# A two-layer encoder trunk: inputs reordered with products of constants ahead of them, right-hand sums made in the up-projections, and late splits of the down-projections put far behind their loads

## The chip, the cores and the metric

The kernel runs on one core of a Trainium2 chip, in one launch. The metric is the device time of that launch in microseconds. A core has five engines with a queue each: PE (TensorE, matmuls), DVE (VectorE), ACT (ScalarE), POOL (GpSimd) and SP (SyncE, which here only issues transfers). An instruction waits at the head of its engine's queue until its inputs are there, and all that stands behind it waits too. Sixteen DMA engines carry the transfers.

## The reference, cut

Two layers over 1024 frames of width 1024, in float32. Each layer adds a mixer and then a gated MLP to the residual stream x. The mixer of layer 0 is stick-breaking attention beside trailing means, that of layer 1 a gated linear recurrence. What the change touches is the beginning of layer 0's mixer (the projection to q and k) and the MLP of both layers:

```python
def conv_ffn(h, w_up, conv_w, conv_b, w_down):
    u = h @ w_up
    up = jnp.pad(u, ((0, 0), (CONV_WIDTH - 1, 0), (0, 0)))
    conv = conv_b
    for j in range(CONV_WIDTH):
        conv = conv + conv_w[j] * up[:, j:j + s]
    a, g = jnp.split(conv, 2, axis=-1)
    return (jax.nn.silu(a) * g) @ w_down

for layer in range(DEPTH):
    x = x + mixer(rms_norm(x, ...), ...)
    x = x + conv_ffn(rms_norm(x, ffn_norm[layer]), ...)
```

`w_up` is 1024 x 5632 and `w_down` 2816 x 1024.

## The kernel before

Activations are kept transposed, channels on the 128 partitions and frames along a row. Every operand of a product is split into a high part (a cast to a shorter format, done by ACT) and a low part (what the cast lost, subtracted by DVE), and every product is three matmuls: high by high, high by low, low by high. Matmuls are 512 columns wide as a rule. The order on PE is the order of the code. On the other engines a scheduler sets it, by its own estimate of time; in the down-projections SP's order too is that of the code.

**The start.** x comes in eight slices of 128 channels. `Norm.add` (L256) splits each one (`h_hi` on ACT, `h_lo` on DVE) and adds its square to `nacc`. `load_split` (L113) fetches the weights of q and k in two halves each, casts (L139) and subtracts (L140, here on POOL). `start_qk` (L765) multiplies slice by slice: twelve matmuls a slice, 96 in all, to four banks. Then `norm.stats` (L286) sums `nacc`, and the projection to the values follows (L417 to L419).

**The up-projections.** 44 tiles of 128 channels in 22 pairs (a, g); a scheme with seven half-size products instead of eight (`winograd`, L880) computes both tiles of a pair. A pair takes seven products P1 to P7 of 12 matmuls each (line L936). DVE empties the banks (L990, L995, L1001, L1005), scales (L964), runs two steps of the convolution (L1039, L1041), forms the next weights' sums (L907 to L910) and subtracts the low parts (L918). The results of two pairs make one block row of the down-projection's right side: `even` holds the first, `ca` the second. B11 and T1 are stored in DRAM after the first pair; B21, B22, T3 (B22 less B12, L1184) and U (B11 less B21, L1183) after the second.

**The down-projections** (`down`, L1199) use the same scheme: products P1, P5, P6, P3, P7, P4, in that order, of eleven steps (j) each, 66 in all, and then a last part with plain products for B21. A step is twelve matmuls at L1266 to four banks. `prep` (L1243) gets a step's operands three steps ahead (`LEAD`): `fetched` loads the right side into `rb` (four buffers), `left` gets the weights (`rs`, `rw`, `ra`) with a sum on DVE where the scheme wants one (L1226, L1229, L1235), and `split_block` (L1193) casts on ACT (L1195) and subtracts on DVE (L1196). The right sides of P6 and P4 are sums, T3 + B11 and T3 + U: `fetched` loads the first one and then POOL issues a second transfer that adds the other one in place (L1213). The last part needs plain weights (`last_left`, called in P6 at j = 2 and 6, and again in the last part) and plain B21 blocks (`last_right`, from P7's j = 8 on); both load and split in one go.

```python
        right = {"P1": ("B11",), "P5": ("T1",), "P6": ("T3", "B11"), "P3": ("B22",), "P7": ("T3",), "P4": ("T3", "U")}
```

Of the kernel before, what the change touches and what calls it, by code (L numbers as in the profile page):

```python
# [12 lines left out]
F32 = mybir.dt.float32  # L13
R32 = mybir.dt.float32r
AF = mybir.ActivationFunctionType
ALU = mybir.AluOpType
# [24 lines left out]
FGROUP = 2  # L41

# [15 lines left out]
def trunk_kernel(  # L58
# [53 lines left out]

    def load_split(src, pool=None, tags=("whi", "wlo", "wraw"), eng=None, nb=2, raw=None, parts=None,  # L113
                   fetched=None):
        srcs = src if isinstance(src, list) else [src]
        n = sum(a.free_size() for a in srcs)
        pool = pool or wpool
        if fetched is not None:
            raw = fetched
        elif raw is None:  # L120
            raw = (pool if len(tags) > 2 else wpool).tile([P, n], F32, tag=tags[2] if len(tags) > 2 else "wraw",
                                                      name="wraw", bufs=2 if "draw" in tags else 1)
        hi = pool.tile([P, n], R32, tag=tags[0], name="whi", bufs=nb)
        lo = pool.tile([P, n], R32, tag=tags[1], name="wlo", bufs=nb)

        def fetch(cs):
            if not isinstance(src, list):
                nc.sync.dma_start(raw[:, cs], src[:, cs])
# [7 lines left out]
        def part(cs):  # L136
            if fetched is None:
                fetch(cs)
            S.copy(hi[:, cs], raw[:, cs])  # L139
# [111 lines left out]
    class Norm:  # L251
        def __init__(self, gain_col, acc_tile, sq_tile, add_eng=None):
            self.col, self.acc_tile, self.sq_tile = gain_col, acc_tile, sq_tile
            self.h, self.add_eng, self.n = [None] * KT, add_eng, 0

        def add(self, x, parts=None, k=None):  # L256
            k = self.n if k is None else k
            self.n += 1
            hi = hpool.tile([P, T], R32, tag="h", name="h_hi")
            lo = hpool.tile([P, T], R32, tag="h", name="h_lo")  # L260
            g = pcol(self.col + k)
            for cs in parts or [slice(0, T)]:
                a = S.activation(hi[:, cs], x[:, cs], AF.Copy, scale=g)
                b = V.scalar_tensor_tensor(lo[:, cs], x[:, cs], g, hi[:, cs].bitcast(F32), op0=ALU.mult,  # L264
                                           op1=ALU.subtract)
            self.last = a.ins, b.ins
            self.h[k] = hi, lo
            if self.n == 1:
                self.acc = self.acc_tile()
                S.activation(self.acc, x, AF.Square)  # L270
                return
            sq = self.sq_tile()
            S.activation(sq, x, AF.Square)
            (self.add_eng or (V if self.n == KT else G)).tensor_tensor(self.acc, self.acc, sq, op=ALU.add)
# [77 lines left out]
    G.memset(ones, 1.0)  # L352
    epsc = const.tile([P, 1], F32, name="epsc")
# [29 lines left out]
    norm = Norm(C_MIXE, lambda: slot(F32, "nacc"), lambda: etile("kl"), V)  # L383
    for k in range(KT):
        xt = slot(F32, "xt")
        if k == 0:
# [18 lines left out]
    def values(half):  # L405
        wt = [load_split(wv[half, c], ep if half == 0 else None, ("ath", "atl") if half == 0 else ("whi", "wlo"))
              for c in range(2)]
# [158 lines left out]
    def pool_in(g, then):  # L566
# [3 lines left out]
        nc.sync.dma_start(praw[g], poolw[g])  # L570
# [209 lines left out]
    v0 = values(0)  # L780
# [230 lines left out]
    def ffn(layer, nm, after, ow, mixt, onward=None):  # L1011
# [107 lines left out]
        for i in range(FT):  # L1119
# [61 lines left out]
            else:  # L1181
# [3 lines left out]
                b2, ut3 = (dram.tile([P, T], F32, tag=f"{n}{layer}_{i}", name=n) for n in ("b2", "ut3"))  # L1185
                nc.sync.dma_start(b2, ca)
                nc.sync.dma_start(ut3, cg)
                blocks[-1].update(B21=b2[:, T0], B22=b2[:, T1], U=ut3[:, T0], T3=ut3[:, T1])
# [4 lines left out]
    def split_block(src):  # L1193
        t = hpool.tile([P, T], R32, tag="h", name="blk")
        S.copy(t[:, 0:512], src)  # L1195
        V.tensor_sub(t[:, 512:T], src, t[:, 0:512].bitcast(F32))  # L1196
        return t

    def down(layer, blocks, ready, after, onward):  # L1199
# [9 lines left out]
        def fetched(tag, src, add=None, bufs=4):  # L1209
# [30 lines left out]

        right = {"P1": ("B11",), "P5": ("T1",), "P6": ("T3", "B11"), "P3": ("B22",), "P7": ("T3",), "P4": ("T3", "U")}

        def prep(n, j):  # L1243
            if n == "P1" and j < len(ready):
                return ready[j]
            rb = fetched("rb", *(blocks[j][b] for b in right[n]))
# [28 lines left out]
        def last_right(js):  # L1275
            raw = hpool.tile([P, T], R32, tag="h", name="b21").bitcast(F32)
            for cs, j in zip(HALVES, js):
                nc.sync.dma_start(raw[:, cs], blocks[j]["B21"])
                hi = dn.tile([P, 512], R32, tag="ra", name="b21h", bufs=NJ)
                lo = dn.tile([P, 512], R32, tag="rs", name="b21l", bufs=NJ)  # L1280
                S.copy(hi, raw[:, cs])
                V.tensor_sub(lo, raw[:, cs], hi.bitcast(F32))
                b21.append((hi, lo))
# [3 lines left out]
        def last_left(r):  # L1287
            parts = []
            big = (hpool, ("wraw", "h", "h"), (1, 16, 16)) if r == KT // 2 - 1 else (wpool, ("wraw", "whi", "wlo"), (1, 2, 2))
            for k0, k1, (pool, tags, nb) in ((0, KT, big), (KT, NJ, (dn, ("r3", "r3h", "r3l"), (1, 2, 2)))):  # L1290
                raw, hi, lo = ((wpool if t == "wraw" else pool).tile([P, (k1 - k0) * P], d, tag=t, name=t, bufs=b)
                               for t, d, b in zip(tags, (F32, R32, R32), nb))
                nc.sync.dma_start(raw.rearrange("p (f k) -> p f k", k=P), odd[:, k0:k1, r * P:(r + 1) * P])
                S.copy(hi, raw)
                V.tensor_sub(lo, raw, hi.bitcast(F32))
                parts += [(hi[:, sl], lo[:, sl]) for sl in (slice(k * P, (k + 1) * P) for k in range(k1 - k0))]
            return parts
# [8 lines left out]
        rows = {}  # L1306
        for i, (n, j) in enumerate(order):
# [37 lines left out]
        for r in range(half):  # L1345
# [4 lines left out]
            if r + 2 < half:  # L1350
                rows[r + 2] = last_left(r + 2)
# [383 lines left out]
```

## Time and profile before

| | |
|---|---|
| three runs | 2197.35, 2199.06, 2202.14 us (median 2199.06) |
| the profiled execution | 2199.35 us; span from first to last instruction 2197.7 us |
| PE, DVE, ACT, POOL busy | 98%, 76%, 50%, 7% of the span |
| moved by DMA | 280.31 MB, 128 GB/s on average |
| first matmul of the start, first matmul of the norm after q and k | 5.95 us, 31.86 us |
| steps of the down-projections | 881.36 to 1071.43 us (layer 0), 1968.50 to 2162.59 us (layer 1) |

A timeline row has an instruction's start, its length, its engine (a q behind the name is the engine's queue), its line, its operation, what it writes and reads, and in brackets how long the engine had stood idle before it and what ended that. Matmul ends are modelled, so their starts are the safer numbers. A window row has its stretch and length, then each engine's busy time with the number of instructions (PE, PEld, DVE, ACT, POOL), the granted TensorE clock, the busy share of the DMA engines and GB/s. A group row has the number of instructions, their busy time and mean length in ns, then the idle time before them and what ended it. A source row has minimum, median and maximum length in ns, then first and last start.

### The profile page before, as it was taken

The numbers are of one execution on the slowest core, as the hardware profiler recorded it, in microseconds if no ns is written. First come the engines' busy times: TensorE is split into PE (matmuls) and PEld (weight loads), VectorE is DVE, ScalarE is ACT, GpSimd is POOL, SyncE is SP. The second block draws the span as 40 slices with busy tenths as digits, with TensorE's granted clock in tenths as the row PEclk, the third lists the DMA queues.
The fourth block names the chain that finished last, engine by engine and source line by source line (L and its number), as shares of the span: only waits on it lengthen the run. The fifth ranks groups of instructions, "written<-read, shape, count | busy, mean of one in ns | idle before, by whom it ended". The sixth has DMA issues, their size and how long they took to land.

```text
span 2197.7 us, 28082 instructions
## 1 busy us (share of the span) xinstructions
PE 2150.8 (98%) x10384; PEld 1767.0 (80%) x10384; DVE 1664.8 (76%) x2458; ACT 1093.1 (50%) x1705; POOL 162.1 (7%) x188
## 2 busy tenths in 40 slices
PE   8999989999999999999999999999999999999998
PEld 7889878888878888778887878787788888887776
DVE  5687688698989899777736655557898998987763
ACT  6666566464444444344546362637544444443441
POOL 2240120000000000010000000000000000000110
PEclk9999999999999999999999999999999999999999
DMA  4132332353444434987501111105343444449885
GB/s 152 49 107 87 94 112 94 119 130 106 130 119 126 124 116 124 350 216 233 169 21 40 38 49 38 49 30 145 105 124 116 123 122 120 124 157 327 222 239 157
DMA packets 126201, 280.31 MB, mean 128 GB/s; under 512 B 13408, under 2 KB 27360, under 8 KB 126064
## 3 DMA queue, kind: packets, MB, share of 16 engines
q1 hardware_dynamic: 112528, 251.25, 34.9%
q0 software_dynamic: 13536, 27.27, 7.0%
q8 instruction: 81, 1.33, 0.2%
q14 instruction: 56, 0.46, 0.1%
HBM read 208.21 MB, written 54.53 MB: 120 GB/s over the span
## 4 chain that ended last, share of the span: by engine, by line
PE 61%; DMA 15%; DVE 15%; issue 4%; ACT 4%; SPq 1%; POOL 0%; DVEq 0%; ACTq 0%; POOLq 0%
PE lin L936 10%; PE z L936 7%; PE lin L153 4%; PE lin L155 4%; PE lin L157 4%; DMA rb<-ut 4%; PE t L936 3%; PE d L936 3%; DMA rw<-in_wdn 3%; DVE blk L1196 2%; PE z L157 2%; PE z L153 2%; PE z L155 2%; DMA raw_g<-in_wup 2%; DMA wraw<-in_wup 2%
## 5 line engine op out<-in xcount | busy, mean ns | idle before, releaser
L1038 ACT ACTIVATE c<-u,prm 128x1024 f32<-128x1024 f32 x88 | 109.1, 1244 | 86.7 <-DVE u L964 79.1
L1266 PE MATMUL lin<-blk 128*128 128x512 f32 x396 | 118.6, 400 | 14.0 <-ACT blk L1195 8.6
L1196 DVE TENSOR_TENSOR blk<-rb,blk 128x512 fp32r<-128x512 f32 x124 | 85.1, 686 | 53.9 <-ACT blk L1195 53.4
L153 PE MATMUL lin<-h_hi,whi 128*128 128x512 f32 x288 | 114.2, 432 | 6.6 <-ACT whi L139 6.0
L1039 DVE SCALAR_TENSOR_TENSOR c<-u,prm,c 128x1023 f32<-128x1023 f32 x88 | 112.3, 1278 | 8.5 <-ACT c L1038 8.5
L1195 ACT CAST blk<-rb 128x512 fp32r<-128x512 f32 x124 | 76.6, 618 | 81.2 <-DMA rb<-ut 44.0
L936 PE MATMUL d<-T,a 128*128 128x512 f32 x480 | 115.4, 389 | 0.0
L1041 DVE SCALAR_TENSOR_TENSOR c<-u,prm,c 128x1022 f32<-128x1022 f32 x88 | 112.3, 1276 | 0.0
L1266 PE MATMUL t<-blk 128*128 128x512 f32 x396 | 112.0, 391 | 0.0
L1266 PE MATMUL d<-blk 128*128 128x512 f32 x396 | 111.9, 391 | 0.0
L1266 PE MATMUL z<-blk 128*128 128x512 f32 x396 | 111.6, 390 | 0.0
L964 DVE TENSOR_TENSOR u<-u,rstd_bc 128x512 f32<-128x512 f32 x160 | 107.8, 684 | 0.4
L936 PEld LDWEIGHTS d<-T,a 128*128 128x128 f32 x480 | 90.1, 188 | 18.7
L155 PE MATMUL lin<-h_lo,whi 128*128 128x512 f32 x288 | 104.4, 398 | 0.7 <-DVE h_lo L264 0.7
L1266 PEld LDWEIGHTS lin<-blk 128*128 128x128 f32 x396 | 73.0, 189 | 39.8 <-ACT blk L1195 13.2
L157 PE MATMUL lin<-h_hi,wlo 128*128 128x512 f32 x288 | 104.2, 398 | 0.0
L936 PE MATMUL z<-blk,s34h 128*128 128x512 f32 x320 | 101.3, 398 | 1.4 <-DVE u L995 1.4
L936 PE MATMUL z<-blk,s12h 128*128 128x512 f32 x320 | 100.9, 396 | 0.0
L936 PE MATMUL lin<-T,s34h 128*128 128x512 f32 x320 | 99.5, 392 | 0.8 <-ACT tm L986 0.8
L936 PE MATMUL t<-blk,whi 128*128 128x512 f32 x320 | 99.6, 392 | 0.0
L936 PE MATMUL lin<-blk,whi 128*128 128x512 f32 x320 | 99.5, 392 | 0.0
L936 PE MATMUL lin<-T,s12h 128*128 128x512 f32 x320 | 99.4, 391 | 0.0
(516 smaller groups left out, 6021.0 us busy)
## 6 DMA issues: line engine op xcount, KB each, us to landing
wraw<-in_wup SPq DMA_DIRECT2D x44, 512.0 KB, 3.7
rw<-in_wdn SPq DMA_DIRECT2D x88, 256.0 KB, 4.7
raw_g<-in_wup SPq DMA_DIRECT2D x40, 512.0 KB, 3.8
rb<-ut SPq DMA_DIRECT2D x66, 256.0 KB, 4.4
b<-c SPq DMA_DIRECT2D x22, 512.0 KB, 2.6
ut<-c SPq DMA_DIRECT2D x22, 512.0 KB, 3.8
s<-in_wup SPq DMA_DIRECT2D x40, 256.0 KB, 2.6
s<-s POOLq DMA_DIRECT2D x40, 256.0 KB, 4.4
```

Source lines behind the costliest of these rows:

```text
L153: PE.matmul(out[i], wh, ah[i], start=first, stop=False)
L155: PE.matmul(out[i], wh, al[i], start=False, stop=False)
L157: PE.matmul(out[i], wl, ah[i], start=False, stop=last)
L936: PE.matmul(ps, w, m, start=first and k == 0 and n == 0, stop=k == 3 and n == 2, skip_group_check=True)
L964: V.tensor_tensor(dst, dst, rstd_bc[:, cs], op=ALU.mult)
L1038: S.activation(c, u, AF.Identity, scale=pcol(b + 2), bias=pcol(b + 3))
L1039: V.scalar_tensor_tensor(c[:, 1:], u[:, :T - 1], pcol(b + 1), c[:, 1:], op0=ALU.mult, op1=ALU.add)
L1041: V.scalar_tensor_tensor(c[:, 2:], u[:, :T - 2], pcol(b), c[:, 2:], op0=ALU.mult, op1=ALU.add)
L1195: S.copy(t[:, 0:512], src)
L1196: V.tensor_sub(t[:, 512:T], src, t[:, 0:512].bitcast(F32))
L1266: PE.matmul(ps, l, m, start=first and j == 0 and i == 0, stop=j == NJ - 1 and i == 2, skip_group_check=True)
```

## The change

**Start.** 24 matmuls of `ones` by `ones` (128x128 in full float32, into a bank that is not read) stand ahead of PE's first product. SP's order is now that of the code: slices 1 and 2 of x stand between the halves of the weights, the convolution's parameters and `cnt` wait until the value weights are fetched. The first halves' low parts are subtracted by DVE instead of POOL, slice 1 is split in halves, and the adds to `nacc` come one slice later.

**Up-projections.** U + T3 (T4) and B11 + T3 (T2) are formed by DVE and stored, T4 in U's place and T2 in a block of its own.

**Down-projections.** P6 and P4 load T2 and T4 in one transfer each. `last_left` and `last_right` only issue loads; what splits them is kept in `due` and called later, behind the latest block's split.

```diff
+    warm = bank("d")
+    for _ in range(WARM):
+        PE.matmul(warm[:, 0:P], ones, ones, start=True, stop=True, skip_group_check=True)
...
-            parts.extend(lambda cs=cs: part(cs) for cs in HALVES)
+            parts.extend(lambda cs=cs, e=e: part(cs, e) for cs, e in zip(HALVES, (V, eng)))
...
-            pq[1]()
-            pk[1]()
+            norm.first = split_ins[0]
         else:
             nc.sync.dma_start(xt, xT[k * P:(k + 1) * P, :])
-        norm.add(xt, HALVES if k == 0 else None)
-    nc.sync.dma_start(prm[:, C_CONV:], par[:, C_CONV:])
-    nc.sync.dma_start(cntc, cnt)
+            if k < 3:
+                (pq, pk)[k - 1][1]()
+        norm.add(xt, HALVES if k < 2 else None)
...
                 V.tensor_tensor(cg[:, T1], ca[:, T1], even[:, T1], op=ALU.subtract)
-                b2, ut3 = (dram.tile([P, T], F32, tag=f"{n}{layer}_{i}", name=n) for n in ("b2", "ut3"))
+                V.tensor_tensor(cg[:, T0], cg[:, T0], cg[:, T1], op=ALU.add)
+                V.tensor_tensor(even[:, T0], even[:, T0], cg[:, T1], op=ALU.add)
...
+                nc.sync.dma_start(t2, even[:, T0])
...
-            if add is not None:
-                G.dma_start(t, add, accum_op=ALU.add)
...
-        right = {"P1": ("B11",), "P5": ("T1",), "P6": ("T3", "B11"), "P3": ("B22",), "P7": ("T3",), "P4": ("T3", "U")}
+        right = {"P1": "B11", "P5": "T1", "P6": "T2", "P3": "B22", "P7": "T3", "P4": "T4"}
...
+        ROWS, LATER = [("P5", 6), ("P3", 1)], [("P6", 6), ("P3", 10)]
...
-            if n == "P6" and j in (2, 6):
-                rows[j // 4] = last_left(j // 4)
-            k = NJ * (n == "P4") + j - 8
-            if n in ("P7", "P4") and k % 2 == 0 and 0 <= k < NJ + 1:
-                last_right(range(k, min(k + 2, NJ)))
+            if (n, j) in LATER:
+                with behind_latest():
+                    due.pop(0)()
+            if (n, j) in ROWS:
+                due.append(last_left(ROWS.index((n, j))))
+            k = NJ * (n == "P4") + j - 2
+            if n in ("P7", "P4") and k % 2 == 0 and 0 <= k < NJ + 5:
+                if k > 3:
+                    with behind_latest():
+                        due.pop(0)()
+                if k < NJ + 1:
+                    due.append(last_right(range(k, min(k + 2, NJ))))
```

How the queues stand now, at three places. First SP at the very start (`xt` are slices of x, `wraw` and `kg` the weights of q and k, `prm` and `cntc` parameters), before:

```order
L347 DMA prm<-in_par 128x44
L391 DMA xt<-in_xT 128x512
L128 DMA wraw<-in_wqk 128x512
L391 DMA xt<-in_xT 128x512
L128 DMA kg<-in_wqk 128x512
L128 DMA wraw<-in_wqk 128x512
L128 DMA kg<-in_wqk 128x512
L398 DMA prm<-in_par 128x352
L399 DMA cntc<-in_cnt 128x64
L396 DMA xt<-in_xT 128x1024 x7
```

The same place on SP in the changed kernel:

```order
L363 DMA prm<-in_par 128x44
L413 DMA xt<-in_xT 128x512
L131 DMA wraw<-in_wqk 128x512
L413 DMA xt<-in_xT 128x512
L131 DMA kg<-in_wqk 128x512
L417 DMA xt<-in_xT 128x1024
L131 DMA wraw<-in_wqk 128x512
L417 DMA xt<-in_xT 128x1024
L131 DMA kg<-in_wqk 128x512
L417 DMA xt<-in_xT 128x1024 x5
L131 DMA wraw<-in_wv 128x1024 x2
L809 DMA prm<-in_par 128x352
```

Slice 1 of x moved from the tenth transfer to the sixth, and the parameters from the eighth to behind the value weights.

Second, DVE in an up-projection, in the second pair of a block row (`u` are a pair's results, `tm` a bank's copy, `s` and `s34l` the next weights), before:

```order
L918 TENSOR_TENSOR a_4345<-raw_g,a_4345 128x512
L1183 TENSOR_TENSOR c<-even,c 128x512
L1184 TENSOR_TENSOR c<-c,even 128x512
L964 TENSOR_TENSOR u<-u,rstd_bc 128x512
L1005 TENSOR_TENSOR u<-tm,z 128x512
L907 TENSOR_TENSOR s_4339<-raw_g 128x512
```

DVE at this place in the changed kernel:

```order
L948 TENSOR_TENSOR a_4375<-raw_g,a_4375 128x512
L1213 TENSOR_TENSOR c<-even,c 128x512
L1214 TENSOR_TENSOR c<-c,even 128x512
L994 TENSOR_TENSOR u<-u,rstd_bc 128x512 x2
L1215 TENSOR_TENSOR c<-c 128x512
L1216 TENSOR_TENSOR even<-even,c 128x512
L937 TENSOR_TENSOR s_4369<-raw_g 128x512
L1035 TENSOR_TENSOR u<-tm,z 128x512
```

The two new adds (L1215 and L1216) stand directly ahead of the weights' next sum and of the emptying of P3's bank (L1035).

Third, DVE at the beginning of P5 (`rs` and `rw` are weights that are summed, `x` takes the banks of P1), before, from the second step's sum on:

```order
L1226 TENSOR_TENSOR rs<-rs,rw 128x512
L1270 TENSOR_TENSOR x<-x,z 128x512
L1270 TENSOR_TENSOR x<-x,t 128x512
L1270 TENSOR_TENSOR x<-x,d 128x512
L1196 TENSOR_TENSOR blk<-rs,blk 128x512
L1196 TENSOR_TENSOR blk<-rb,blk 128x512
L1226 TENSOR_TENSOR rs<-rs,rw 128x512
```

DVE at the beginning of P5 in the changed kernel, from the second step's sum on:

```order
L1268 TENSOR_TENSOR rs<-rs,rw 128x512
L1230 TENSOR_TENSOR blk<-rs,blk 128x512
L1230 TENSOR_TENSOR blk<-rb,blk 128x512
L1311 TENSOR_TENSOR x<-x,lin 128x512
L1271 TENSOR_TENSOR rs<-rs,ra 128x512
L1311 TENSOR_TENSOR x<-x,z 128x512
L1311 TENSOR_TENSOR x<-x,t 128x512
L1311 TENSOR_TENSOR x<-x,d 128x512
L1268 TENSOR_TENSOR rs<-rs,rw 128x512
```

The adds to x moved from between the second step's sum and its blocks to between those blocks and the third step's sum. In P5's middle four steps still have the sequence block, block, `rs` less `ra`, `rs` plus `rw`. At the end of P5 and in P6, SP now has the late weights ahead of the loads of P5's last step, and then eleven loads of one block each:

```order
L1339 DMA wraw<-in_wdn 128x8x128
L1339 DMA r_8077<-in_wdn 128x3x128
L1255 DMA rb<-t_7493 128x512
L1255 DMA rs<-in_wdn 128x512
L1255 DMA rw<-in_wdn 128x512
L1255 DMA rb<-t_4964 128x512
```

Where the late weights stood before, SP had this (the `ut` blocks hold T3 for P6; POOL's adding transfers are in its own queue):

```order
L1211 DMA rb<-ut_6253 128x512
L1293 DMA wraw<-in_wdn 128x8x128
L1293 DMA r_8168<-in_wdn 128x3x128
L1211 DMA rb<-ut_6514 128x512
L1211 DMA rb<-ut_6775 128x512
```

The loads of late weights moved out of P6, and the loads of sums in P6 became loads of T2 without a second transfer. On PE nothing but the 24 matmuls is new.

More of the change, by code (lines that the diff above doesn't have):

```diff
@@ L269, in add @@
                 self.acc = self.acc_tile()
-                S.activation(self.acc, x, AF.Square)
+                with tc.issue_after(self.first) if self.first is not None else ExitStack():
+                    S.activation(self.acc, x, AF.Square)
                 return
@@ L273, in add, with add_up @@
             S.activation(sq, x, AF.Square)
-            (self.add_eng or (V if self.n == KT else G)).tensor_tensor(self.acc, self.acc, sq, op=ALU.add)
+            def add_up():
+                (self.add_eng or (V if self.n == KT else G)).tensor_tensor(self.acc, self.acc, sq, op=ALU.add)
+            if self.first is None:
+                add_up()
+                return
+            if self.n > 2:
+                with tc.issue_after(b.ins):
+                    self.due()
+            self.due = add_up
+            if self.n == KT:
+                add_up()
         def behind(self):
@@ L778, in start_qk @@
         yield None
-    v0 = values(0)
+    v0 = values(0, value_weights(0))
+    inputs_in = split_ins[1]
+    with tc.issue_after(inputs_in):
+        nc.sync.dma_start(prm[:, C_CONV:], par[:, C_CONV:])
+        nc.sync.dma_start(cntc, cnt)
     fl = Filler()
@@ L1245, in prep @@
                 return ready[j]
-            rb = fetched("rb", *(blocks[j][b] for b in right[n]))
+            rb = fetched("rb", blocks[j][right[n]])
             if n == "P1":
@@ L1278, in last_right, with later @@
                 nc.sync.dma_start(raw[:, cs], blocks[j]["B21"])
[L1279 to L1283, printed above, removed]
+            def later():
+                for cs, j in zip(HALVES, js):
+                    hi = dn.tile([P, 512], R32, tag="ra", name="b21h", bufs=NJ)
+                    lo = dn.tile([P, 512], R32, tag="rs", name="b21l", bufs=NJ)
+                    S.copy(hi, raw[:, cs])
+                    V.tensor_sub(lo, raw[:, cs], hi.bitcast(F32))
+                    b21.append((hi, lo))
@@ L1285, in down @@
+            return later
         odd = wdn[layer].rearrange("(f two) p k -> two p f k", two=2)[1]
         def last_left(r):
-            parts = []
             big = (hpool, ("wraw", "h", "h"), (1, 16, 16)) if r == KT // 2 - 1 else (wpool, ("wraw", "whi", "wlo"), (1, 2, 2))
+            raws = []
             for k0, k1, (pool, tags, nb) in ((0, KT, big), (KT, NJ, (dn, ("r3", "r3h", "r3l"), (1, 2, 2)))):
-                raw, hi, lo = ((wpool if t == "wraw" else pool).tile([P, (k1 - k0) * P], d, tag=t, name=t, bufs=b)
-                               for t, d, b in zip(tags, (F32, R32, R32), nb))
+                raw = (wpool if tags[0] == "wraw" else pool).tile([P, (k1 - k0) * P], F32, tag=tags[0], name=tags[0], bufs=1)
@@ L1293, in last_left, with later @@
                 nc.sync.dma_start(raw.rearrange("p (f k) -> p f k", k=P), odd[:, k0:k1, r * P:(r + 1) * P])
[L1294 to L1297, printed above, removed]
+                raws.append((raw, pool, tags, nb))
+            def later():
+                parts = []
+                for raw, pool, tags, nb in raws:
+                    n = raw.free_size()
+                    hi, lo = (pool.tile([P, n], R32, tag=t, name=t, bufs=b) for t, b in zip(tags[1:], nb[1:]))
+                    S.copy(hi, raw)
+                    V.tensor_sub(lo, raw, hi.bitcast(F32))
+                    parts += [(hi[:, sl], lo[:, sl]) for sl in (slice(k * P, (k + 1) * P) for k in range(n // P))]
+                rows[r] = parts
@@ L1299, in down @@
+            return later
         LEAD = 3
@@ L1305, in down @@
         half = KT // 2
-        rows = {}
+        rows, due = {}, []
+        ROWS, LATER = [("P5", 6), ("P3", 1)], [("P6", 6), ("P3", 10)]
         for i, (n, j) in enumerate(order):
@@ L1350, in down @@
             if r + 2 < half:
[L1351 removed]
+                last_left(r + 2)()
             if r == 0:
```

43 lines of the change are left out of this document (30 added, 13 removed).

## The prediction, before the run

> **What bounds the kernel now.** I read the page's busy line first, then the waits of PE, then PE's timeline at the places that those waits name.
>
> ```profile
> span 2197.7 us, 28082 instructions
> PE 2150.8 (98%) x10384; PEld 1767.0 (80%) x10384; DVE 1664.8 (76%) x2458; ACT 1093.1 (50%) x1705; POOL 162.1 (7%) x188
> PE lin L1266 <- ACT blk L1195: 8.6, 10, 2.1
> PE lin L153 <- ACT whi L139: 6.0, 1, 6.0
> PE lin L1266 <- DVE blk L1196: 5.4, 18, 0.8
> ```
>
> PE is busy for 2150.8 of 2197.7 us. The change removes no product, so only PE's 46.9 us of idle time, and stretches in which it runs below its pace, can be won. The three largest waits (total, times, longest) lie at the two places that the change touches: the down-projections, where PE waits for ACT and DVE to split operands (8.6 and 5.4 us), and the very start (6.0 us).
>
> The down-projections run 66 steps in each layer, P1, P5, P6, P3, P7 and P4 with 11 each. A step opens with three `lin` matmuls; here are first steps of some products, with start and length:
>
> ```profile
> 911.30 0.84 PE L1266 MATMUL lin<-blk 128*128 128x512 f32 x3
> 914.02 1.07 PE L1266 MATMUL lin<-blk 128*128 128x512 f32 x3
> 943.80 0.84 PE L1266 MATMUL lin<-blk 128*128 128x512 f32 x3
> 970.39 0.50 PE L1266 MATMUL lin<-blk 128*128 128x512 f32 x1 [2.08 <-ACT blk L1195]
> 980.81 0.84 PE L1266 MATMUL lin<-blk 128*128 128x512 f32 x3
> 1040.65 0.84 PE L1266 MATMUL lin<-blk 128*128 128x512 f32 x3
> 1068.55 0.84 PE L1266 MATMUL lin<-blk 128*128 128x512 f32 x3
> 1998.47 0.84 PE L1266 MATMUL lin<-blk 128*128 128x512 f32 x3
> 2030.41 0.84 PE L1266 MATMUL lin<-blk 128*128 128x512 f32 x3
> 2066.53 0.84 PE L1266 MATMUL lin<-blk 128*128 128x512 f32 x3
> 2126.37 0.84 PE L1266 MATMUL lin<-blk 128*128 128x512 f32 x3
> 2159.71 0.84 PE L1266 MATMUL lin<-blk 128*128 128x512 f32 x3
> ```
>
> An undisturbed step of twelve matmuls takes 914.02 − 911.30 = 2.72 us, so eleven take 29.92. P5 runs from 911.30 to 943.80 in layer 0 and from 1998.47 to 2030.41 in layer 1: 2.58 and 2.02 us too long. P6, until 980.81 and 2066.53, takes 37.01 and 36.12: 7.09 and 6.20 too long. The first ten steps of P4 (27.20 due) take 27.90 and 33.34: 0.70 and 6.14 too long. P6 and P4 are the products whose right side is fetched and then summed by a second transfer that POOL issues.
>
> ```profile
> 900.00:930.00 30.00, 29.55 (x127) 23.30 (x126) 21.51 (x35) 9.14 (x16) 0.00 (x0) 1.00 1.04 397
> 940.00:970.00 30.00, 26.86 (x114) 20.81 (x112) 16.56 (x25) 11.80 (x20) 7.81 (x9) 1.00 0.94 212
> 943.80:980.80 37.00, 33.24 (x133) 25.70 (x132) 22.48 (x35) 17.11 (x30) 7.09 (x9) 0.95 0.93 225
> 966.54 1.05 ACT L1294 CAST whi<-wraw 128x1024 fp32r<-128x1024 f32 x1 [1.38 <-DMA wraw<-in_wdn]
> 969.72 0.62 ACT L1195 CAST blk<-rb 128x512 fp32r<-128x512 f32 x1 [2.13 <-DMA rb<-b]
> ```
>
> The last three columns of a window are granted clock, busy share of the DMA engines and GB/s. In P5 they move 397 GB/s at share 1.04; in P6, with the summing transfers, 212 at almost the same share. ACT stands first at a split of late weights (`wraw`), then at a block whose sum has not landed, and each is in front of all later blocks.
>
> **The change, part by part.** *P6 and P4.* The sums T2 and T4 are now made by DVE before the blocks are stored. The 44 POOL transfers and the 44 first loads that they waited for become 44 plain loads. The late weights' splits stand 11 and 9 steps behind their loads instead of directly behind, those of `b21` four steps. What made P6 and P4 late is gone from the queues, and the DMA share in P6 should halve (one 256 KB load a step). P7, which has two loads a step and the same splits, runs without loss between the rows above: P3 and P7 together are 59.84 us for 22 steps, exactly 22 × 2.72. I take the whole loss as won: 7.09 + 6.20 + 0.70 + 6.14 = **−20.1 us**; the other end is that half of it stays, −10. The 0.95 clock of P6 is in it: PE's halt is what precedes it.
>
> *P5.* It gains no cover: its loss comes from the order on DVE.
>
> ```profile
> 910.61 0.69 DVE L1226 TENSOR_TENSOR rs<-rs,rw 128x512 f32<-128x512 f32 x1 [0.46 <-DMA rw<-in_wdn]
> 921.33 0.69 DVE L1196 TENSOR_TENSOR blk<-rs,blk 128x512 fp32r<-128x512 f32 x1 [0.76 <-ACT blk L1195]
> 921.94 0.68 DVE L1196 TENSOR_TENSOR blk<-rb,blk 128x512 fp32r<-128x512 f32 x1
> 922.54 0.68 DVE L1229 TENSOR_TENSOR rs<-rs,ra 128x512 f32<-128x512 f32 x1
> 923.15 0.68 DVE L1226 TENSOR_TENSOR rs<-rs,rw 128x512 f32<-128x512 f32 x1
> 924.60 0.69 DVE L1196 TENSOR_TENSOR blk<-rs,blk 128x512 fp32r<-128x512 f32 x1 [0.77 <-ACT blk L1195]
> ```
>
> Four operations at a pitch of 0.60, then 0.76 of waiting while ACT casts the sum: a lap of 924.60 − 921.33 = 3.27 us against PE's 2.72. The new order keeps four such laps, and puts the four adds that drain P1's banks *behind* the blocks of P5's second step and ahead of the third's sum. From 910.61 that gives 0.60 + 0.76 + 1.20 (second step's blocks), five operations (3.0), then 0.60 + 0.76 + 1.28: 918.6 to 918.8, where PE is ready at 911.30 + 2 × 2.72 = 916.74. With the laps behind it P5 loses some 4.6 us in layer 0, and some 2.4 in layer 1, where the same sum starts with a microsecond more in hand. Against today: **+2.4 us** together. Ends: −4.6 (nothing lost any more) and +4. The load of the late weights (704 KB, 1.8 us at 397 GB/s) now falls on P5's end; it stands before the last step's loads, which I take as covered by the three steps of lead.
>
> *Up-projections.* DVE gets two adds of 128x512 for every second tile, 11 pairs in each layer, 44 in all.
>
> ```profile
> 480.00:870.00 390.00, 389.12 (x1685) 315.87 (x1684) 351.24 (x429) 179.38 (x206) 16.37 (x19) 1.00 0.40 120
> L1005 DVE TENSOR_TENSOR u<-tm,z 128x512 f32<-128x512 f32 x19 | 13.0, 686 | 19.0 <-PE z L936 19.0
> 670.93 0.69 DVE L1005 TENSOR_TENSOR u<-tm,z 128x512 f32<-128x512 f32 x1 [1.43 <-PE z L936]
> ```
>
> At 0.60 each they are 13.2 us a layer, 26.4 in all. DVE is busy 351.24 of 390 us there, but it stands idle 19.0 us at L1005, waiting for PE, and the new order puts the adds right in front of that wait: 1.20 of work into a hole of 1.43 in the quoted tile. The extra store (256 KB per pair) meets a DMA share of 0.40. The ends are 0 and +26.4; I take **+1.0**, near the covered end, for the last pair, which now meets the first blocks of P1. What waits behind a late add is the next tile's evacuation, then PE at its bank.
>
> *The start.*
>
> ```profile
> 0.95 0.21 POOL L352 MEMSET ones<- 128x128 f32 x1
> L300 PE MATMUL z<-nsq,ones x4: 592/592/592, 1124.3 to 1125.6; 128*128 128x512 f32 x4
> 5.95 1.58 PE L153 MATMUL lin<-h_hi,whi 128*128 128x512 f32 x2 [5.95 <-ACT whi L139]
> 8.46 1.06 PE L157 MATMUL lin<-h_hi,wlo 128*128 128x512 f32 x2
> 9.31 0.82 PE L153 MATMUL t<-h_hi,whi 128*128 128x512 f32 x2
> 9.97 0.62 PE L155 MATMUL t<-h_lo,whi 128*128 128x512 f32 x2
> 10.43 0.61 PE L157 MATMUL t<-h_hi,wlo 128*128 128x512 f32 x2
> 13.11 0.73 PE L155 MATMUL lin<-h_lo,whi 128*128 128x512 f32 x2 [0.72 <-DVE h_lo L264]
> 31.86 1.84 PE L286 MATMUL d<-ones,nacc 128*128 128x2 f32 x16
> ```
>
> The first products run from 5.95 to 31.86, 25.9 us for 96 matmuls that take 8 × 2.72 = 21.8 at full pace. A pair takes 0.85 us at 8.46 and 0.46 at 9.97, so PE runs at half pace until about 3.8 us after its first matmul; then come two waits for the second slice of x. The 24 new matmuls in full precision are free to start at 1.16, when `ones` is set. Four records of 512 columns start within 1.3 us (0.43 each), and a matmul is two records; a quarter as wide that is 0.21 a matmul, or 0.43 at half pace. If PE speeds up 3.8 us after they begin, nine run slow and fifteen fast: they end at 1.2 + 3.8 + 3.2 = 8.2. The first products then start 2.2 us later than today but run unbroken, since the second slice now stands sixth instead of tenth among the loads: they end at 30.0, 1.9 earlier. The ends are a block all fast (6.3, a gain of 3.8) and all slow (11.5, a loss of 1.4). I take **−1.5**, with 0.4 for waits that I do not see.
>
> The Trainium skill, "TensorE: Matmul & The Clock Gate", Part 1, "What's actually happening", says that the clock opens after a free-running window of about 3.4 us filled with activity. By that rule the block would end, as an estimate, between 8.1 and 9.8, and the sum would come out up to 1.6 us later; the 3.8 us of this trace fit it.
>
> The sum is made against the profiled execution, 2199.35 us (its span and 1.65 around it), which is 0.3 above the median of 2199.06: 2199.35 − 20.1 + 2.4 + 1.0 − 1.5 = **2181.2**, so 2181.
>
> **Rivals.** *The wait moves within the down-projections.* P5 already moves 397 GB/s and gets 704 KB more; the splits that moved could stop ACT elsewhere. Against it: P3, P7 and most of P1 carry such loads without a loss. It would give half the 20.1 back: 2191.
>
> *DVE becomes the bound of the up-projections; slower.* If the holes at L1005 only look free, because the tile's other work is then late, every pair costs its 1.2 us: 2181.2 − 1.0 + 26.4 = 2206.6. It decides as soon as uncovered adds exceed 18 us, 0.8 a pair. Against it: DVE's busy share only rises from 90% to 93%.
>
> *The warming block does not do what it says* and ends at 11.5: the start costs 1.4 instead of winning 1.5, 2184.
>
> *P5's losses vanish as well*, because the splits come at better moments than the order tells: 2181.2 − 2.4 − 4.6 = 2174.
>
> **How the numbers follow.** Forecast 0.70, moved wait 0.13, DVE bound 0.07, late block 0.05, better P5 0.05. The range from 2174 to 2190 takes in the forecast with the ends of P5 and of the start, the late block, the better P5 and the milder half of the moved wait; it leaves out the rest of that and the DVE bound. About 0.2% (4.4 us) is what a measurement of this kernel can tell from no change. Faster: 0.70 + 0.05 + 0.05 + half of 0.13, 0.87; the same: the other half and a little of the DVE case, 0.07; slower: 0.06.
>
> **What would show it.** Right: P6 and P4 at 2.72 us a step, no POOL transfers there, P5 still at 3.27 in its middle, PE's first row near 1.2 and the norm's matmuls near 30. Wrong: PE waits for `u` (L995, L1005's places) in the up-projections, an ACT wait for `wraw` in the down-projections, or a first product that starts after 10 us.

## The result, and the profile after

Four runs of the changed kernel took 2172.44 to 2179.16 us, median 2177.57, beside four of the kernel before at 2195.56 to 2202.14, median 2198.2. The ratio is 0.9901, 95% interval 0.9878 to 0.9924: about 21 us faster. The profiled execution took 2179.16 us, 20.2 less than the one before. The forecast was 2181.0.

The page's busy lines and the largest waits of PE (total, times, longest), after:

```profile
span 2177.5 us, 28146 instructions
PE 2146.3 (99%) x10432; PEld 1771.5 (81%) x10432; DVE 1693.9 (78%) x2505; ACT 1093.5 (50%) x1706; POOL 122.1 (6%) x142
PE d L782 <- DVE atl L770: 3.8, 7, 1.0
PE lin L156 <- DVE o_b L597: 2.2, 1, 2.2
PE t L302 <- DVE nsq L357: 2.0, 1, 2.0
PE z L966 <- DVE u L1025: 1.8, 2, 1.0
PE lin L1307 <- DVE blk L1230: 1.2, 5, 0.3
```

The down-projections (now L1307) led this list with 8.6 and 5.4 us; 1.2 us are left. One wait is new, 2.0 us for the sum of squares in layer 1's MLP norm. The up-projections' waits for `u` are 1.8 us; they were 1.4. PE's timeline at first steps of P5, P6, P3 and P4, layer 0 and then layer 1:

```profile
906.23 0.84 PE L1307 MATMUL lin<-blk 128*128 128x512 f32 x3
937.64 0.84 PE L1307 MATMUL lin<-blk 128*128 128x512 f32 x3
967.56 0.84 PE L1307 MATMUL lin<-blk 128*128 128x512 f32 x3
1027.40 0.84 PE L1307 MATMUL lin<-blk 128*128 128x512 f32 x3
1054.60 0.84 PE L1307 MATMUL lin<-blk 128*128 128x512 f32 x3
...
1990.67 0.84 PE L1307 MATMUL lin<-blk 128*128 128x512 f32 x3
2022.43 0.84 PE L1307 MATMUL lin<-blk 128*128 128x512 f32 x3
2052.35 0.84 PE L1307 MATMUL lin<-blk 128*128 128x512 f32 x3
```

P6 takes 967.56 − 937.64 = 29.92 us and 29.92 in layer 1: eleven times 2.72, nothing lost. Ten steps of P4 take 27.20, nothing lost. P5 takes 31.41 and 31.76, 1.49 and 1.84 too long. By stages, from one matmul's start to another's (us in the profiled executions):

| stage | before | after | difference |
|---|---|---|---|
| start and mixer of layer 0, to the first product of the up-projections | 492.05 | 486.83 | −5.2 |
| up-projections, layer 0 | 389.31 | 389.43 | +0.1 |
| P1's first to P4's last matmul, layer 0 | 189.69 | 180.83 | −8.9 |
| last part, mixer of layer 1, start of its MLP | 507.18 | 514.15 | +7.0 |
| up-projections, layer 1 | 390.28 | 389.46 | −0.8 |
| P1's first to P4's last matmul, layer 1 | 193.70 | 181.18 | −12.5 |
| from there to the end | 35.45 | 35.57 | +0.1 |

The down-projections win 21.4. What the mixer of layer 0 wins, the stretch to layer 1's MLP loses again, and neither was in the forecast at that size.

### The profile page after: what moved, and what is told of

It is laid out like the page before. It is cut to its first block, busy times and chain, and to the rows that moved or that the text cites. A ratio compares the mean times of both kernels' runs of the same rounds, so it can differ in the third digit from the quotient of the medians.

```text
span 2177.5 us, 28146 instructions
## 1 busy us (share of the span) xinstructions
PE 2146.3 (99%) x10432; PEld 1771.5 (81%) x10432; DVE 1693.9 (78%) x2505; ACT 1093.5 (50%) x1706; POOL 122.1 (6%) x142
## 5 line engine op out<-in xcount | busy, mean ns | idle before, releaser
L1307 PE MATMUL lin<-blk 128*128 128x512 f32 x396 | 113.2, 391 | 1.3 <-DVE blk L1230 1.2
L1307 PE MATMUL z<-blk 128*128 128x512 f32 x396 | 111.3, 389 | 0.0
L1307 PE MATMUL t<-blk 128*128 128x512 f32 x396 | 111.2, 389 | 0.0
L1307 PE MATMUL d<-blk 128*128 128x512 f32 x396 | 111.2, 389 | 0.0
L142 ACT CAST whi<-wraw 128x1024 fp32r<-128x1024 f32 (+2 forms) x57 | 57.1, 1002 | 74.7 <-PE z L158 21.8
L1307 PEld LDWEIGHTS lin<-blk 128*128 128x128 f32 x396 | 73.8, 188 | 19.1 <-DVE blk L1230 4.1
L1229 ACT CAST blk<-rw 128x512 fp32r<-128x512 f32 x66 | 41.0, 621 | 94.1 <-DVE rw L1279 42.1
```

The lines of the kernel that those rows point to most:

```text
L142: split_ins[0] = S.copy(hi[:, cs], raw[:, cs]).ins
L1229: a = S.copy(t[:, 0:512], src)
L1307: PE.matmul(ps, l, m, start=first and j == 0 and i == 0, stop=j == NJ - 1 and i == 2, skip_group_check=True)
```

## The experiments

**Sums alone and late splits alone.** The first is the kernel before with T2 and T4 in the up-projections and one load a block; the second is the kernel before with the late splits only.

```diff
 sums_only, against the kernel before
+                V.tensor_tensor(cg[:, T0], cg[:, T0], cg[:, T1], op=ALU.add)
+                V.tensor_tensor(even[:, T0], even[:, T0], cg[:, T1], op=ALU.add)
...
-            if add is not None:
-                G.dma_start(t, add, accum_op=ALU.add)
...
+        right = {"P1": "B11", "P5": "T1", "P6": "T2", "P3": "B22", "P7": "T3", "P4": "T4"}
```

> The kernel before with one part of the change alone: T2 and T4 are formed in the up-projections, and P6 and P4 load one block a step; late weights and B21 blocks are split directly behind their loads, as before, and the start is as before. If the summing transfers made P6 and P4 late (theory A), P6 takes 29.9 to 30.5 us in each layer and P4 no more, nearly all of the 20.1 us is won, and the time is 2178 to 2181. If it was the splits that stood directly behind their loads (rival B), P6 and P4 keep at least half of their loss, and the time is 2189 or more. Where ACT waits for the late weights, P6 may lose some tenths under either.

Measured: 2175.96 us (2173.95 to 2179.31) beside 2195.92 for the kernel before, ratio 0.9906 (0.9885 to 0.9928): the 20 us of theory A, from a lower base than I took. P6 and P4 lose nothing in either layer, with the late weights split directly behind their loads. P5 loses 2.97 and 1.37 us.

```diff
 late_only, against the kernel before
+            if (n, j) in LATER:
+                with behind_latest():
+                    due.pop(0)()
+            if (n, j) in ROWS:
+                due.append(last_left(ROWS.index((n, j))))
```

> The kernel before with the other part alone: late splits of weights and B21 blocks stand far behind their loads, but T2 and T4 are still summed by POOL's second transfers. Theory A: P6 keeps at least 5 of its 7.09 and 6.20 us, P4 of layer 1 at least 4 of its 6.14, and the time is 2194 to 2199. Rival B: ACT no longer stops, P6 and P4 lose less than half of what they lost, and the time is 2189 or less.

Measured: 2195.26 us (2190.81 to 2198.37, ten runs), ratio 0.9991 (0.9978 to 1.0003), no difference that can be told. In its profiled execution, the fastest of the ten, P6 still loses 3.5 and 3.3 us and P4 3.9 and 5.6, against 7.1, 6.2, 0.7 and 6.1 before. That P6 would keep at least 5 us in each layer was wrong. ACT's timeline in layer 1's P4 (`rb` are right sides whose sum POOL's transfer makes):

```profile
2125.26 0.62 ACT L1212 CAST blk<-rb 128x512 fp32r<-128x512 f32 x1 [2.32 <-DMA rb<-ut]
2128.91 0.62 ACT L1212 CAST blk<-rb 128x512 fp32r<-128x512 f32 x1 [2.51 <-DMA rb<-ut]
2141.45 0.62 ACT L1212 CAST blk<-rb 128x512 fp32r<-128x512 f32 x1 [6.26 <-DMA rb<-ut]
```

With no late split in front of it, ACT still stands at a sum that has not landed, up to 6.26 us. Theory A holds, by the run before this one above all: without the summing transfers P6 and P4 lose nothing. The late splits took half of P6's loss away in this one profile while those transfers were there, gave some of it back in P4, and win nothing once the transfers are gone.

**The old start in the changed kernel.**

```diff
 no_start, against the changed kernel
-    for _ in range(WARM):
-        PE.matmul(warm[:, 0:P], ones, ones, start=True, stop=True, skip_group_check=True)
...
-            if k < 3:
-                (pq, pk)[k - 1][1]()
+            pq[1]()
+            pk[1]()
```

> The changed kernel with the start as before (order of the inputs, no warming block, first halves split by POOL). By the prediction's term the time is 1.5 us above the changed kernel's 2177.6, 2179. The profile of the changed kernel shows 0.8 us kept at 61 us and another 4.3 between 219 and 282 us, where two stretches at half clock are gone. If those hang on the start (rival), they come back here and the time is 2182 to 2183; if they vary from run to run, this profile may show either and the time stays near 2179.

Measured: 2177.63 us (2174.13 to 2178.83), ratio 0.9907 (0.9882 to 0.9932): the start's worth does not show in the time. In its profile the first up-projection product starts at 491.93, as before, with four stretches at half clock ahead of it.

**No warming block**, the order of loads kept (`WARM = 0`), beside a second profile of the changed kernel.

> The changed kernel without the 24 matmuls ahead of the first product; the order of loads stays. If the warm clock is what the start gained by, the first products run at half pace from 5.95 until some 3.8 us later, and the norm's matmuls begin 1.5 to 2 us later than 30.64. If the operands of the later slices set the end (ACT is busy without a hole from 7.12 on, and PE's one wait in the start was for slice 3's low part), the norm's matmuls begin within 0.4 us of 30.64 and the time is the changed kernel's within 0.5.

> The changed kernel a second time, beside the next three. If the loss of 6.6 us around 1540 us (a wait of 1.05 for the blocks, one of 1.96 for the squares' sum, then 6.8 us at half clock) belongs to the kernel, it stands in this profile too and the time is 2177 to 2180; if it comes from how the adding transfers of the norm happen to fall, it may be gone, with a time near the fastest run, 2172.

Measured: 2175.29 us (2173.88 to 2178.3) without the block, 2173.85 (2172.2 to 2180.14) for the changed kernel. PE's timeline, first product and norm, without the block:

```profile
6.00 1.55 PE L156 MATMUL lin<-h_hi,whi 128*128 128x512 f32 x2 [6.00 <-ACT whi L142]
31.29 1.84 PE L302 MATMUL d<-ones,nacc 128*128 128x2 f32 x16
```

The same with it, the changed kernel's first profile:

```profile
1.20 7.16 PE L372 MATMUL d<-ones 128*128 128x128 f32 x48 [1.20 <-POOL ones L368]
8.12 0.72 PE L156 MATMUL lin<-h_hi,whi 128*128 128x512 f32 x2
17.35 0.73 PE L158 MATMUL lin<-h_lo,whi 128*128 128x512 f32 x2 [0.31 <-DVE h_lo L267]
30.64 1.84 PE L302 MATMUL d<-ones,nacc 128*128 128x2 f32 x16
```

The norm starts 0.65 us later without the block: between my two cases, nearer to the one in which the operands set the end. Of the start's 1.22 us (31.86 to 30.64) the order of loads makes 0.57, the block 0.65; these are single profiles. In the changed kernel's second profile the first product starts at 8.68 and the norm at 30.62, in its third at 9.25 and 31.15, so that there the block is worth 0.14. The wait for the squares' sum (1.98 us, at 1545.41) stood in the second profile of the changed kernel too.

**P5: subtractions held back, side loads moved, both.** P5's remaining loss looked like the lap of DVE. The first edit holds P6's subtraction behind the last but one block, the second issues the four loads of x and the late weights behind P5's own loads, the third is both.

```diff
 p5_defer, against the changed kernel
             if n == "P6":
-                V.tensor_tensor(s[j], s[j], a11[j], op=ALU.subtract)
+                with tc.issue_after(prior[1]):
+                    V.tensor_tensor(s[j], s[j], a11[j], op=ALU.subtract)
 p5_loads, against the changed kernel
-            if n == "P5" and j < 4:
-                load_x(half + j)
+            if n == "P5" and j >= 7:
+                load_x(half + j - 7)
-        ROWS, LATER = [("P5", 6), ("P3", 1)], [("P6", 6), ("P3", 10)]
+        ROWS, LATER = [("P5", 10), ("P3", 1)], [("P6", 6), ("P3", 10)]
```

> The changed kernel, with P6's subtraction (rs less ra) held on DVE until behind the last but one block, so that P5's lap is block, block, sum and the wait for the cast: 3 x 0.60 + 0.76 = 2.56 us instead of 3.27. If the lap sets P5's pace, P5 takes 29.9 us in both layers (1.49 and 1.84 lost today) and the time falls by 3.3 us against the changed kernel beside it. Rival: the subtractions make P6 late instead, since its lap grows from 1.2 to 1.8 us of work beside the drain of P5's banks; then P6 loses 1 to 3 us and the time does not fall.

> The changed kernel with P5's side loads moved alone: the four loads of x that stood in P5's first four steps, and the late weights (704 KB) that stood at its seventh, are issued behind P5's last own loads; P6's subtractions stay where the scheduler puts them. If DVE's lap of 3.27 us by itself sets P5's pace (theory lap), P5 still loses 1.1 to 1.9 us in each layer, and the time is the changed kernel's. If the loads do (theory loads), P5 takes 29.9 and the time falls by 3.

> Both edits at once: P6's subtractions held back, and P5's side loads behind its own. With the subtractions held back alone, DVE's lap became 2.66 us, but DVE then waited for rw six times in P5 and P5 lost 1.57 and 1.44 us still. If lap and loads were two bounds one behind the other, P5 now takes 29.9 us in both layers, P6 at most 0.3 more, and the time is 3.0 to 3.5 us below the changed kernel's, 2171 to 2174 by the medians. Rival: the loads of x now land while DVE already stands at the drain of P5's banks, P6 loses what P5 wins, and the time does not fall.

Measured: p5_defer 2176.0 us (2174.43 to 2178.79), p5_loads 2174.86 (2172.18 to 2177.63), p5_both 2175.63 (2170.42 to 2180.1). P5 loses 1.57 and 1.44 us with the subtractions held back, 0.00 and 1.13 with the loads moved, nothing with both. DVE's timeline in P5, subtractions held back:

```profile
913.91 0.69 DVE L1230 TENSOR_TENSOR blk<-rs,blk 128x512 fp32r<-128x512 f32 x1 [0.77 <-ACT blk L1229]
...
916.71 0.69 DVE L1268 TENSOR_TENSOR rs<-rs,rw 128x512 f32<-128x512 f32 x1 [1.51 <-DMA rw<-in_wdn]
```

The lap is shorter by the subtraction, but then `rw` is not there, and P6 now loses 0.23 us in each layer. The sums of P5 wait for it four times in each layer, 0.48 to 1.51 us. With the loads moved as well, one sum a layer waits inside P5, 0.15 to 0.63 us in two profiles, and PE loses nothing. So behind the lap stands a second bound, the loads. (DVE's order is not quite the same in the two runs; this is read from the waits.) PE's first steps of P5, P6 and P3 with both edits, in both layers:

```profile
908.85 0.84 PE L1308 MATMUL lin<-blk 128*128 128x512 f32 x3
938.77 0.84 PE L1308 MATMUL lin<-blk 128*128 128x512 f32 x3
968.69 0.84 PE L1308 MATMUL lin<-blk 128*128 128x512 f32 x3
...
1984.92 0.84 PE L1308 MATMUL lin<-blk 128*128 128x512 f32 x3
2014.84 0.84 PE L1308 MATMUL lin<-blk 128*128 128x512 f32 x3
2044.76 0.84 PE L1308 MATMUL lin<-blk 128*128 128x512 f32 x3
```

Each is 29.92 us.

What p5_loads says of the loads is less than it seems, because the edit to SP's queue also moved DVE's sums, whose place the scheduler sets. In the changed kernel a middle lap of P5 ends with the sum and then a wait for ACT's cast of it:

```profile
917.00 0.69 DVE L1268 TENSOR_TENSOR rs<-rs,rw 128x512 f32<-128x512 f32 x1
918.44 0.69 DVE L1230 TENSOR_TENSOR blk<-rs,blk 128x512 fp32r<-128x512 f32 x1 [0.76 <-ACT blk L1229]
```

In p5_loads the sum stands between the two blocks:

```profile
913.60 0.69 DVE L1230 TENSOR_TENSOR blk<-rs,blk 128x512 fp32r<-128x512 f32 x1 [0.16 <-ACT blk L1229]
914.20 0.69 DVE L1268 TENSOR_TENSOR rs<-rs,rw 128x512 f32<-128x512 f32 x1
914.81 0.68 DVE L1230 TENSOR_TENSOR blk<-rb,blk 128x512 fp32r<-128x512 f32 x1
915.41 0.68 DVE L1271 TENSOR_TENSOR rs<-rs,ra 128x512 f32<-128x512 f32 x1
916.01 0.68 DVE L1230 TENSOR_TENSOR blk<-rs,blk 128x512 fp32r<-128x512 f32 x1
```

All four operations are still in the lap, but the wait is gone: 916.01 − 913.60 = 2.41 us instead of 3.26 (915.18 to 918.44). That is below PE's 2.72, so layer 0's 0.00 can come from this order alone; in the changed kernel's middle laps no sum waits for `rw`. Layer 1's 1.13 falls on the third and fourth steps, behind a second sum that waited 1.46 us for `rw`. The run does not decide between the theories of its expectation.

**Twice the new adds.** Two more adds per pair, into a block that nobody reads.

```diff
 double_adds, against the changed kernel
                 V.tensor_tensor(even[:, T0], even[:, T0], cg[:, T1], op=ALU.add)
+                V.tensor_tensor(even[:, T1], cg[:, T0], cg[:, T1], op=ALU.add)
+                V.tensor_tensor(even[:, T1], even[:, T0], cg[:, T1], op=ALU.add)
```

> The changed kernel with two more adds of 128x512 per pair of the up-projections, whose results nobody reads: DVE gets another 13.2 us a layer. It tests how far the cover reaches that the prediction counted on (19.0 us of waits for PE per 390 us, of which the first two adds take 13.2). If the cover is what it looks like, the four adds (26.4 a layer) overrun it by some 7 us a layer at the most, and the up-projections end 2 to 14 us later in all. If the adds had been free because DVE has slack anywhere, the time stays within 1 us; if each uncovered add counts in full, it rises by 26.

Measured: 2182.66 us (2179.3 to 2189.58), some 5 above what the changed kernel took in other sets of runs, but not where I expected it. The up-projections take 389.53 and 389.52 us, as with two adds. The down-projections take 2.3 and 3.5 longer, all of it in P5. SP's and DVE's timelines ahead of P5 in layer 0 (P5 starts at 911.40), then PE's in layer 1:

```profile
880.25 0.32 SPq L1208 DMA_DIRECT2D b<-even  x1
906.34 0.69 DVE L1270 TENSOR_TENSOR rs<-rs,rw 128x512 f32<-128x512 f32 x1 [1.29 <-DMA rw<-in_wdn]
```

```profile
1992.86 0.84 PE L1309 MATMUL lin<-blk 128*128 128x512 f32 x3
1997.58 0.49 PE L1309 MATMUL lin<-blk 128*128 128x512 f32 x1 [1.85 <-ACT blk L1231]
```

A step of P5 takes 1997.58 − 1992.86 = 4.72 us there. In the body of the up-projections even 26.4 us of adds a layer are covered; the end is what costs, and P5 pays. It does not pay by DVE's time there: DVE stands idle for `rw`, 1.29 us just before the first sum. `rw` is late by SP's queue. SP stands at the store of the last `even` (L1208) until DVE has made it, 31.15 us ahead of P5 in this kernel. In the changed kernel that is 33.50:

```profile
872.73 0.32 SPq L1208 DMA_DIRECT2D b<-even  x1
```

P5's loads stand behind that store, and the second step's `rw` is issued 8.42 us ahead of P5 instead of 11.44. This is read from the rows.

**Third profile, second profile of the version with both edits, and additions on POOL.** The last edit replaces the adding transfers of layer 1's MLP norm.

```diff
 pool_adds, against the version with both edits
-                G.dma_start(self.part, sq, accum_op=ALU.add)
+                if self.layer:
+                    G.tensor_tensor(self.part, self.part, sq, op=ALU.add)
+                else:
+                    G.dma_start(self.part, sq, accum_op=ALU.add)
```

> The changed kernel a third time, with five timed runs, beside the next two on the same chip. From the end of layer 0's down-projection losses to layer 1's first up-projection matmul the trace takes either 686.5 us (seven of eleven profiles) or 690 to 693 (four, with the adding transfers of the squares 6.0 us apart instead of 5.1). If this hangs on the kernel, the profile shows the long form a third time; if it is chance, either. The time is 2173 to 2179.

> The changed kernel with P6's subtractions held back and P5's side loads behind its own, a second time. In the first profile all six products ran at 2.72 us a step in both layers. If that is worth what the trace shows, the median is 3 us (1.5 to 4.5) below that of the changed kernel beside it; if the losses of P5 come back elsewhere, it is within 1.

> The version with both edits, and layer 1's MLP norm with its five sums of squares added by POOL itself (128x1024) instead of by adding transfers. If the chain of adding transfers is what sometimes costs 4 to 7 us around 1540, the wait for the squares' sum is gone and the stretch takes 686 us in every run, so the time is 2170 to 2173 and its spread smaller. Rival: POOL's additions slow DVE beside them (at the start a subtraction of POOL took 2.17 instead of 1.29 us and DVE's next to it 2.23 instead of 1.27), DVE is busy there all the time, PE waits, and the time is 2175 or more.

Measured, beside each other: the changed kernel 2178.92 us (2171.95 to 2180.27), both edits 2174.84 (2169.65 to 2180.45), POOL's additions 2179.93 (2177.49 to 2182.55). The ratios to the kernel before, 0.9903 (0.9883 to 0.9923), 0.9892 (0.9867 to 0.9916) and 0.9913 (0.9894 to 0.9931), overlap. The version with both edits has the lower median here and, over all its eleven runs, 2175.63 against 2177.9 of fourteen of the changed kernel, over several chips; in both its profiles the down-projections are 3.3 us shorter. It would be the version to take, but the time does not separate it from the changed kernel. DVE's timeline with POOL's additions:

```profile
1505.10 5.02 DVE L331 SCALAR_TENSOR_TENSOR blk<-x,prm,blk 128x512 fp32r<-128x512 f32 x2
1510.04 2.90 DVE L991 TENSOR_TENSOR x<-x 128x512 f32<-128x512 f32 x1
1512.86 0.74 DVE L331 SCALAR_TENSOR_TENSOR blk<-x,prm,blk 128x512 fp32r<-128x512 f32 x1
```

and POOL's beside it:

```profile
1503.98 8.41 POOL L353 TENSOR_TENSOR nacc<-nacc,nsq 128x1024 f32<-128x1024 f32 x3 [18.86 <-ACT nsq L348]
```

While POOL's three additions run, 2.8 us each, an operation of DVE that takes 0.74 alone takes 2.5 (5.02 for two). PE then waits 4.3 us for DVE's and ACT's blocks between 1531 and 1539, and the stretch up to layer 1's up-projections takes 515.7 us, where the version with both edits takes 507.3 and 507.7. The rival was right; POOL cannot add there for nothing. The Trainium skill, "SBUF — State Buffer", "Who interferes with whom", says that a DVE instruction with two SBUF inputs and a POOL instruction that reads SBUF share a port by an exclusive lock; these rows agree.

## Why the prediction was right

**P6 and P4, −20.1.** Right in place and size: every step is 2.72 us (−7.09, −6.20, −0.70, −6.14). Of the two causes that the text named, only one carried it: sums alone win all, late splits alone nothing measurable. That the DMA share in P6 should halve was wrong: it is 0.75 against 0.93, by the window row of the changed kernel's P6.

```profile
937.60:967.50 29.90, 29.90 (x133) 24.75 (x133) 25.66 (x42) 16.26 (x29) 0.00 (x0) 1.00 0.75 232
```

**P5, +2.4.** Here the prediction failed. It was −1.3: 3.33 us lost instead of 4.60. The laps of 3.2 to 3.3 came as read (PE's eighth to tenth steps start at 925.73, 928.94 and 932.20 in layer 0), but what they start from was wrong: I kept the second step's sum at its old time, 0.69 us ahead of P5, and laid the laps behind it. It ran far earlier. DVE's timeline after:

```profile
902.15 0.69 DVE L1268 TENSOR_TENSOR rs<-rs,rw 128x512 f32<-128x512 f32 x1
907.81 0.69 DVE L1268 TENSOR_TENSOR rs<-rs,rw 128x512 f32<-128x512 f32 x1
```

The second sum stands 4.08 us ahead of P5 (906.23), the third at 907.81, although the drain is in front of it. In layer 1 the second stands 3.73 us ahead.

That the order costs about what I read, and only its start was off, the other profiles show. In all that have the new order and leave P5's queues alone (three of the changed kernel, sums_only, no_start, warm0, double_adds), P5's loss and the second sum's lead on P5 add up to the same in either layer, 5.56 to 5.61 us and once 5.74. In the two with the old order (before, late_only) they add up to 3.25 to 3.29. So the new order costs 2.3 us a layer at an equal lead, and the changed kernel loses less than before only because its sums lead by 2.5 to 3.4 us more. With the old lead of 0.69 us this gives 4.9 us in layer 0, where I had 4.6. My 2.4 for layer 1 does not follow from my own working: before, the second sum led there by 1.23 us, 0.54 more than in layer 0 and not a microsecond, which leaves 4.1.

A part of the reason for the longer lead is in SP's queue, which I had read for P6 but not here. Before:

```profile
902.84 0.32 SPq L1187 DMA_DIRECT2D ut<-c  x1
904.03 0.33 SPq L1211 DMA_DIRECT2D rw<-in_wdn  x1
```

After:

```profile
894.79 0.33 SPq L1255 DMA_DIRECT2D rw<-in_wdn  x1
896.76 0.33 SPq L1220 DMA_DIRECT2D t<-c  x1
```

The last pair's store stood ahead of the second step's `rw`; two adds later it stands behind it, and `rw` is issued 11.4 us ahead of P5 instead of 7.3. The store's place is not the whole reason. In sums_only and no_start it stands behind `rw` too, yet in layer 0 the second sum leads by only 2.59 and 2.91 us and P5 loses 2.97 and 2.65, no less than before. With the new order the second sum follows the first by some 3.3 us, a lap, and the first waits for its own `rw`. In layer 0 that landed 5.93 and 6.26 us ahead of P5 in these two, 7.57 in the changed kernel and 5.16 with twice the adds. What lets it land earlier stays open, and no run put the store alone back.

That the lead would cover the late weights' load was right: P5's loss falls between the first matmuls of its sixth and its tenth step in both layers, at the laps, and its last two steps, with that load in the queue, lose nothing.

**Up-projections, +1.0.** In this pair of profiles +0.1 and −0.8. The wait for the last pair came as forecast (1.0 us at 873.36, 0.8 at 1957.81). It stands in both layers of every profile with the adds, 0.35 to 1.05 us long, and in none without them. Four waits of before (0.9 at 609.62, 0.8 at 1590.23, 0.2 and 0.3 later) are gone, but such waits come and go in other profiles with and without the adds. Against late_only, which has no adds and takes 388.7 and 389.4 us, the changed kernel takes 0.8 more in the two layers together. So the profiles do not settle the sign of a term of this size. The rival that DVE becomes the bound is refuted beyond its own terms: twice the adds cost the up-projections nothing.

**The start, −1.5.** −1.22 at the norm. The block ended at 8.12 (8.2 forecast), and at 8.68 and 9.25 in the second and third profile. So the 3.8 us at half pace was one draw of several. The rule of the Trainium skill, "TensorE: Matmul & The Clock Gate", Part 1, "What's actually happening", gave 8.1 to 9.8 by the prediction's estimate, and these profiles agree. As 8.2 + 21.8 and 5.95 + 1.9 + 21.8 come to almost the same end, the prediction's own sum should have told me that the block was worth little.

**What was not in it.** The first stretch won 5.2 and the fourth lost 7.0. Against the forecast P5 is 3.7 us better, the up-projections 1.7 and the first stretch 3.7, and the fourth is 7.0 worse. The total is right by P6 and P4, and beyond that by luck, as these four nearly cancel. In the first stretch the number of half-clock stretches differs: before had four ahead of the up-projections, this profile one. Two window rows around 255 us, first before, then after (granted clock third from the end):

```profile
230.00:280.00 50.00, 47.56 (x258) 40.25 (x257) 29.98 (x58) 29.52 (x55) 7.16 (x3) 0.93 0.29 82
```

```profile
230.00:280.00 50.00, 48.27 (x283) 41.12 (x283) 33.79 (x65) 31.11 (x60) 7.17 (x3) 1.00 0.36 108
```

Over all profiles the up-projections begin at 489.5 to 492.1 with the old start (four) and at 486.8 to 491.9 with the new one (ten). The changed kernel's own three begin at 486.8, 490.4 and 488.9. So the start wins between nothing and 5 us there, and which it is changes from run to run.

In the fourth stretch POOL's adding transfers of layer 1's norm are issued 6.0 us apart or more instead of 5.1 to 5.5, ACT waits for the buffer that they free, the squares' sum is late, and PE drops to half clock for 6.83 us:

```profile
1530.56 1.06 ACT L348 ACTIVATE nsq<-x 128x1024 f32<-128x1024 f32 x1 [3.99 <-DMA nacc<-nsq]
1542.61 2.46 PE L302 MATMUL t<-ones,nsq 128*128 128x2 f32 x16 [1.96 <-DVE nsq L357]
1543.87:1550.70 6.83, 6.83 (x21) 5.57 (x21) 6.83 (x11) 4.23 (x6) 0.85 (x1) 0.50 0.43 109
```

All three profiles of the changed kernel have this, with 3.41 or 6.83 us at half clock (514.2, 512.2 and 511.6 us for the stretch), and so have p5_defer and p5_loads (510.7, 512.9). Both profiles of the version with both edits do not (507.3, 507.7), nor do warm0, double_adds and the four with the old start (506.1 to 507.3). Whether it hangs on the build or on the execution stays open. The profiled executions of the changed kernel took 2178.8 to 2180.1 us and those of the version with both edits 2171.5 and 2171.6, but each kernel also ran at the other's time: the changed one at 2171.95, the other at 2180.45.

## What to carry to other kernels

Where two causes stand in one queue, a transfer that lands late and work that waits in front of it, undo them one at a time: here only the transfer mattered, and moving the work behind it bought nothing. When an edit lengthens a chain of work, follow its stores through the queue that loads the next stage's operands; extra work may move a store out of the way or into it, and the price can show a stage later than the work itself. A loss by one bound can hide the next one a few tenths behind it, so change both before judging either by the time. Where a scheduler sets the order, read every engine's order again after an edit to one queue: moving loads on SP also moved DVE's sums, and so the run did not test the loads alone.

## What the runs showed of the hardware

- Half-clock stretches come in units of 3.41 us (3.41 or 6.83 in every profile but at the very end), each about 1.7 us of PE's work lost. With one of them the up-projections began at 486.8 and 486.9, with two at 486.9 to 489.5, with three at 488.1, with four at 490.4 to 492.1, with five at 491.9. The length of a wait alone does not say whether one follows: before, PE waits 1.6 us for `atl` at 241.1 and a stretch begins at 241.8, but in late_only the same wait at 241.8 is followed by none.
- The same kernel's runs spread over 8 to 11 us (2169.65 to 2180.45 for the version with both edits), several times what the profiles' stage differences of 1 to 3 us need to be seen. Such sizes are read from the trace or not at all.
- An adding transfer costs the DMA engines more than a plain one of the same size: P6 moved 225 GB/s at share 0.93 with them and 232 at 0.75 without.
